# A Strassen-Winograd decoder step on 8 cores: new load order at the start, a gate/up epilogue without POOL, other weight slots, scheduler margins, and a reordered last stage before the odd mixer and the end

## The chip, the cores and the metric

The kernel runs on all 8 cores of one Trainium2 chip. Each core does the same work on its own data, and no core talks to another. The metric is the device time of the slowest core, in microseconds (us). Cores 0 to 3 are on one die, 4 to 7 on the other.

The program has a slower state that came in some executions: the cores of one die showed a lower granted TensorE clock than the others, and the time was some per cent longer. This document compares fast runs with fast runs only.

## The reference

One step of a two-layer decoder: a prompt group (8 sequences of 2048) and a sample group (128 sequences of 8 new tokens) share all weights.

```python
for layer in range(2):
    x = x + 0.5 * swiglu(rmsnorm(x), w_gate, w_up, w_down)      # FFN 1 (layer 0), FFN 3 (layer 1)
    h = rmsnorm(x)
    if layer == 0: m = even_mixer(h)     # chunked spatial gating || short gated convolution
    else:          m = odd_mixer(h)      # causal pooling over windows 2, 4, 8, 16
    x = x + m
    x = x + 0.5 * swiglu(rmsnorm(x), ...)                       # FFN 2, FFN 4
y = rmsnorm(x)
# D_MODEL 1024, D_FF 2816; swiglu(h) = (silu(h @ w_gate) * (h @ w_up)) @ w_down
```

Each core has one prompt sequence and 16 sample sequences, 2176 columns in all. They are handled as four token blocks of 544 columns. An FFN does two blocks at a time ("first half", "second half").

## The kernel before

Nearly all of the work is bf16 matmuls of 272 columns. Each 2x2 block of an FFN product is done with the seven products of Strassen-Winograd, M1 to M7, so DVE must form sums of weights ("S", four per weight item) and differences of activations ("T") before TensorE can use them.

```python
PARTS = [(0, 6), (6, 8), (14, 8)]     # the three column parts of a half of an FFN
def weight_sums(wt, n):               # 4 DVE operations of 128x1024 (gate/up): the "S" sums
    ...
def tsums(buf, o):                    # 3 DVE operations per 4 stored tiles: the "T" differences
    ...
```

Weights go through three slots of SBUF. A load into a slot can start only when the item that lay there has been released, so the assignment of items to slots, and the order of the cells that use them, decide how early a load starts.

```python
            k = (0, 0, 2, 0)[2 * l + w]
            for half in range(2):
                for pi, (f0, nf) in enumerate(PARTS):
                    for f in range(f0, f0 + nf, 2):
                        items.append((("gu", l, w, f, half), 4096, W0 + SLOT * (k % 3), SLOT))
                        k += 1
                    for q in range(2):
                        items.append((("dn", l, w, pi, q, half), nf * 512, W0 + SLOT * (k % 3), SLOT))
                        k += 1
                if (l, w, half) == (0, 1, 0):
                    k += 1
# ... in ffn(): the order of the gate/up cells (weight item i, token block t) of the last part
                if pi == 2:
                    cells[-6:] = [(i, t) for t in range(2) for i in range(n - 3, n)]
```

The epilogue of a gate/up cell (X is gate, Y is up). Two of the four products gate*up are formed by POOL:

```python
            X_.prod(7, X_.c, False)
            t22 = X_.sum5(X_.c)               # DVE: SBUF <- PSUM + M5
            X_.prod(3, X_.b, False)
            t12 = X_.sum5(X_.b)
            give(X_.b)
            Y_.prod(7, Y_.c, False)
            u22 = Y_.sum5(Y_.c)
            Y_.prod(3, Y_.b, False)
            u12 = Y_.sum5(Y_.b)
            give(Y_.b)
            act_silu(t=t22)
            act_silu(t=t12)
            self.put(B22, t22, u=u22)         # POOL: SBUF <- SBUF * SBUF
            self.put(T2B, t12, u=u12)         # POOL
```

A norm squares eight chunks on ACT, adds them on POOL, and sums over partitions with one TensorE matmul against ones. The `Down` cells at the end of an FFN go output half by output half (q outer, token block t inner).

The order of instructions on every engine is not written by hand. A list scheduler in the program simulates all engines with a cost formula for each operation, gives each operation a latest start LS worked out backwards from an ideal, gapless TensorE, and picks, with a few exceptions, the available operation with the smallest LS:

```python
            LS[i] = f - (issue(o) + dma_t(o) if o.ndma else o.cost)
            # ... when operation i has been placed, each successor s becomes ready:
                ready_t[s] = max(ready_t[s], o.end + self.lat(o, ops[s]))
```

At the start, the SP queue issues the four quarters of the first token block of x, and the small constants (norm gains) after them.

## Time and profile before

The median was 2232.51 us (4 runs, 2231.01 to 2233.3). The busy part of the page of the kernel before, core 0 (span, share of it, instructions):

```profile
span 2230.6 us, 53049 instructions; the slowest of 8 cores (2212.9 to 2230.6 us)
PE 2098.6 (94%) x16680; PEld 1631.1 (73%) x16712; DVE 1566.0 (70%) x3372; ACT 1228.9 (55%) x3070; POOL 987.4 (44%) x1150
```

TensorE is the limit: 2098.6 of 2230.6 us. What a change to other engines can win is the idle time of PE. The waits of PE in the kernel before name it, by the line of the waiting matmul and by what it waited for (total us, times, longest us). L785 is the main matmul, L1428 and L703 the norm sums, L662 the mixers' matmuls; L618 is the S sums, L756 the T differences, "arena<-wall" a weight load, L723 the multiplication that makes h, L905 the addition to x.

```profile
PE ps L1428 <- ACT accr L1426: 17.7, 3, 7.9
PE ps L703 <- POOL accr L693: 16.4, 10, 3.4
PE ps L785 <- DVE arena L618: 15.2, 12, 2.5
PE ps L785 <- DVE arena L756: 13.1, 8, 5.1
PE ps L785 <- DMA arena<-wall: 9.8, 8, 2.4
...
PE ps L662 <- DVE arena L723: 9.4, 3, 6.1
PE ps L785 <- DVE xT L905: 7.0, 12, 1.7
...
```

The following lines of the PE timeline of the kernel before (start, length, line, matmuls, and in brackets the idle time before them and its releaser) show places that the change aims at: the start (to 70 us), the weight loads near 950 us, and the norm before the odd mixer (1635 us).

```profile
27.34 1.83 PE L1428 MATMUL ps<-accr,onesr 128*128 128x272 f32 x5 [5.61 <-DVE accr L1423]
35.98 1.07 PE L785 MATMUL ps<-arena 128*128 128x272 bf16 x4 [5.07 <-DVE arena L756]
69.98 1.07 PE L785 MATMUL ps<-arena 128*128 128x272 bf16 x4 [3.69 <-DVE arena L723]
...
945.72 8.32 PE L785 MATMUL ps<-arena 128*128 128x272 bf16 x56 [2.03 <-DMA arena<-wall]
956.45 4.61 PE L785 MATMUL ps<-arena 128*128 128x272 bf16 x24 [2.41 <-DMA arena<-wall]
...
1635.79 4.41 PE L662 MATMUL ps<-arena 128*128 128x384 bf16 x16 [6.15 <-DVE arena L723]
```

The end, in the DVE timeline of the kernel before: all 16 multiplications of the last two token blocks stand in a row at the end, after the last main matmul (2210 us). The last matmul of all, a norm sum, ended at 2216.3 us.

```profile
2211.74 12.83 DVE L723 SCALAR_TENSOR_TENSOR xT<-xT,misc,arena 128x544 f32<-128x544 f32 x16 [1.10 <-ACT arena L713]
```

Two groups of the kernel before: POOL's multiplications, from the page, and the S sums on DVE, from the list of groups by form (count, busy us, mean ns, then idle time before and its releasers). DVE's own multiplications of this kind, 352 of them, took 437 ns.

```profile
L858 POOL TENSOR_TENSOR arena<-arena 128x272 bf16<-128x272 f32 x352 | 274.6, 792 | 681.8 <-ACT arena L840 476.6
```

```profile
L618 DVE TENSOR_TENSOR arena<-arena 128x1024 bf16<-128x1024 bf16 x240 | 197.0, 847 | 19.7 <-DMA arena<-wall 17.9
```

### The profile page before, as it was taken

What the parts mean: (1) busy time and instruction counts of PE and PEld (TensorE: products, weight loads), DVE (VectorE), ACT (ScalarE), POOL (GpSimd) and SP (SyncE); (2) the same over time, 40 slices, a digit from 0 to 9 for tenths busy, and PEclk for the clock granted to TensorE, in tenths of its full rate; (3) what the DMA queues carried; (4) which work ended last, traced back from release to release, by engine and by line L of the source; (5) the groups of instructions that cost most, each with busy time, mean ns of one, the idle gap of its engine ahead of it and who ended that gap; (6) DMA issues with size and microseconds to landing.
All of it is one profiled execution on the core that took longest, in us unless ns stands there. A gap on an engine that the chain in (4) does not pass through costs nothing.

```text
span 2230.6 us, 53049 instructions; the slowest of 8 cores (2212.9 to 2230.6 us)
## 1 busy us (share of the span) xinstructions
PE 2098.6 (94%) x16680; PEld 1631.1 (73%) x16712; DVE 1566.0 (70%) x3372; ACT 1228.9 (55%) x3070; POOL 987.4 (44%) x1150
## 2 busy tenths in 40 slices
PE   4799999999999999999999999999989999999995
PEld 3688788874555888778887887888744688878874
DVE  4777965577557877955587879655666887886665
ACT  3655565557334555555555555655565555555554
POOL 2633463356206423453345334633566533264325
PEclk9999999999999999999999999999999999999998
DMA  8587656561321676646555776565621277567563
GB/s 214 122 173 163 163 136 165 133 129 30 58 36 48 141 181 152 172 105 165 135 124 118 178 162 173 131 158 133 149 58 49 58 172 161 139 160 177 136 184 113
DMA packets 56290, 298.69 MB, mean 134 GB/s; under 512 B 7120, under 2 KB 11472, under 8 KB 31824
## 3 DMA queue, kind: packets, MB, share of 16 engines
q0 software_dynamic: 21600, 132.92, 35.7%
q1 hardware_dynamic: 34416, 162.38, 20.7%
q8 instruction: 140, 2.29, 0.4%
q14 instruction: 134, 1.10, 0.2%
HBM read 347.90 MB, written 80.28 MB: 192 GB/s over the span
## 4 chain that ended last, share of the span: by engine, by line
PE 75%; DVE 8%; DMA 5%; issue 5%; POOL 4%; ACT 2%; DVEq 0%; SPq 0%; POOLq 0%; ACTq 0%
PE ps L785 64%; PE ps L662 11%; DMA arena<-wall 3%; POOL arena L693 2%; DVE arena L723 2%; DVE arena L831 1%; DMA misc<-cst 1%; DVE arena L618 1%; DVE arena L756 1%; DVE arena L759 1%; DVE xT L905 1%; DMA arena<-scrgu 1%; POOL xT L925 1%; DVE xT L723 1%; ACT ps L806 0%
## 5 line engine op out<-in xcount | busy, mean ns | idle before, releaser
L785 PE MATMUL ps<-arena 128*128 128x272 bf16 x14784 | 1747.6, 281 | 62.1 <-DVE arena L618 15.2
L785 PEld LDWEIGHTS ps<-arena 128*128 128x128 bf16 x14784 | 1440.7, 98 | 365.0 <-issue 93.2
L806 ACT ACTIVATE ps<-ps 128x272 f32<-128x272 f32 x1088 | 416.7, 383 | 398.5 <-PE ps L785 237.1
L858 POOL TENSOR_TENSOR arena<-arena 128x272 bf16<-128x272 f32 x352 | 274.6, 792 | 681.8 <-ACT arena L840 476.6
L905 DVE SCALAR_TENSOR_TENSOR xT<-ps,xT 128x272 f32<-128x272 f32 x768 | 310.9, 435 | 138.2 <-PE ps L785 123.0
L662 PE MATMUL ps<-arena 128*128 128x512 bf16 (+2 forms) x1736 | 335.0, 351 | 14.3 <-DVE arena L723 9.4
L925 POOL TENSOR_TENSOR xT<-xT,arena 128x544 f32<-128x544 f32 x192 | 256.1, 1339 | 136.6 <-ACT arena L817 66.1
L831 DVE TENSOR_TENSOR arena<-ps,arena 128x272 f32<-128x272 f32 x704 | 294.2, 437 | 29.0 <-PE ps L785 16.3
L693 POOL TENSOR_TENSOR arena<-arena 128x272 f32<-128x272 f32 (+3 forms) x288 | 249.7, 873 | 118.1 <-DVE arena L723 28.4
L662 PEld LDWEIGHTS ps<-arena 128*128 128x128 bf16 x1768 | 171.6, 98 | 168.6 <-issue 17.6
L854 DVE TENSOR_TENSOR arena<-ps,arena 128x272 bf16<-128x272 f32 x352 | 153.7, 437 | 184.9 <-ACT ps L806 113.9
L840 ACT ACTIVATE arena<-arena 128x272 f32<-128x272 f32 x352 | 144.7, 427 | 196.4 <-DVE arena L831 191.8
L685 ACT ACTIVATE arena<-xT 128x272 f32<-128x272 f32 (+3 forms) x336 | 153.0, 457 | 163.2 <-POOL arena L693 95.3
L817 ACT ACTIVATE arena<-ps 128x272 f32<-128x272 f32 x544 | 214.4, 394 | 41.4 <-PE ps L785 26.1
L618 DVE TENSOR_TENSOR arena<-arena 128x1024 bf16<-128x1024 bf16 (+1 forms) x272 | 219.9, 833 | 21.3 <-DMA arena<-wall 19.4
L756 DVE TENSOR_TENSOR arena<-arena 128x544 bf16<-128x544 bf16 x240 | 127.7, 544 | 118.3 <-POOL arena L858 118.3
L723 DVE SCALAR_TENSOR_TENSOR arena<-xT,misc,arena 128x544 bf16<-128x544 f32 (+4 forms) x216 | 187.0, 895 | 7.5 <-ACT arena L713 3.9
L604 POOL DMA_DIRECT2D arena<-wall x148 | 87.0, 588 | 227.7 <-PE ps L785 104.4
L759 DVE TENSOR_TENSOR arena<-arena 128x272 bf16<-128x272 bf16 x480 | 157.0, 344 | 15.1
L840 ACT ACTIVATE arena<-ps 128x272 f32<-128x272 f32 x352 | 139.2, 395 | 14.3 <-PE ps L785 1.8
L1172 DVE TENSOR_TENSOR xT<-ps,xT 128x512 f32<-128x512 f32 (+2 forms) x80 | 48.2, 606 | 36.2 <-PE ps L662 35.9
L693 POOL TENSOR_TENSOR accr<-arena 128x272 fp32r<-128x272 f32 (+3 forms) x48 | 41.5, 864 | 10.2 <-DVE arena L756 2.7
(78 smaller groups left out, 532.9 us busy)
## 6 DMA issues: line engine op xcount, KB each, us to landing
arena<-wall POOLq DMA_DIRECT2D x68, 1024.0 KB, 10.4
arena<-wall POOLq DMA_DIRECT2D x72, 768.0 KB, 8.8
scrgu<-arena SPq DMA_DIRECT2D x44, 1024.0 KB, 8.9
arena<-scrgu SPq DMA_DIRECT2D x44, 1024.0 KB, 6.8
scrdn<-arena SPq DMA_DIRECT2D x16, 1024.0 KB, 7.6
arena<-scrdn SPq DMA_DIRECT2D x16, 1024.0 KB, 6.1
y<-xT SPq DMA_DIRECT2D x8, 1088.0 KB, 6.9
xT<-x SPq DMA_DIRECT2D x6, 1088.0 KB, 14.2
```

The source lines that it names most:

```text
L618: P.add("dve", lambda e, dst=dst, x=x, y=y, op=op: e.tensor_tensor(out=wt(*s(dst)), in0=wt(*s(x)), in1=wt(*s(y)), op=op), r=[wt.key(*s(x)) ...
L662: ins = e.matmul(banks[bk][:, 0:n], l, rr, start=(i == 0), stop=(i == len(pairs) - 1), skip_group_check=True)
L693: P.add("pool", lambda e: e.tensor_tensor(out=o, in0=acc(0, n), in1=q(0, n), op=ALU.add), r=[q.key(0, n), acc.key(0, n)], w=[ok], c=c_p(n))
L723: P.add("dve", lambda e: e.scalar_tensor_tensor(out=dst, in0=xc(c, a, n), scalar=g, in1=rs(a, a + n), op0=ALU.mult, op1=ALU.mult), r=[xck( ...
L785: ins = e.matmul(banks[bk][:, 0:N2], l, rr, start=fresh and kc == 0, stop=kc == self.nk - 1, skip_group_check=True)
L806: P.add("act", lambda e: e.activation(out=banks[dst][:, 0:N2], in_=banks[src][:, 0:N2], func=AF.Copy), r=[("ps", src)], w=[("ps", dst)], c ...
L817: P.add("act", lambda e: e.activation(out=s(0, N2), in_=banks[e_][:, 0:N2], func=AF.Copy, scale=0.5 if self.half else 1.0), r=[("ps", e_)] ...
L831: P.add("dve", lambda e: e.tensor_tensor(out=t(0, N2), in0=banks[bk][:, 0:N2], in1=s(0, N2), op=ALU.add), r=[("ps", bk), s.key(0, N2)], w= ...
L840: P.add("act", lambda e: e.activation(out=t(0, N2), in_=i_, func=AF.Silu), r=[r], w=[t.key(0, N2)], c=c_a(N2), tab="silu")
L858: P.add("pool", lambda e: e.tensor_tensor(out=m7(p, p + N2), in0=u(0, N2), in1=t(0, N2), op=ALU.mult), r=[u.key(0, N2), t.key(0, N2)], w=[ ...
L905: P.add("dve", lambda e: e.scalar_tensor_tensor(out=xc(dc, a, N2), in0=banks[bk][:, 0:N2], scalar=0.5, in1=xc(dc, a, N2), op0=ALU.mult, op ...
L925: P.add("pool", lambda e, dc=dc, a=a, s=s: e.tensor_tensor(out=x3[:, dc:dc + 2, a:a + N2], in0=x3[:, dc:dc + 2, a:a + N2], in1=s(0, N2).un ...
```

## The change

The change has six parts.

1. **Start.** The constants are loaded first, the second block of x is held until the first weights have landed, the later blocks until the third weight item has, and two stores of weight sums are held.
2. **Epilogue.** POOL's 352 multiplications go to DVE, which reads them from PSUM. For that the up-side sum is written back to PSUM.
3. **Weight slots and cell order.** Another slot map, and the last part of a half takes its last two items (not three) token block by token block.
4. **Margins.** The scheduler treats results that pass between engines (those for TensorE excepted) as ready up to 0.5 (ACT), 0.8 (DVE) or 1.5 us (POOL) later than computed, at most a quarter of the slack, so that it makes orders less tight.
5. **Before the odd mixer.** The last `Down` cells go token block by token block; of the last two token groups' eight squares, squares 4 to 7 are summed by TensorE directly rather than by POOL; three chunks of the mixer are interleaved at its start (two before); the pooling weights are loaded earlier.
6. **End.** The same token-major `Down` and direct sums in the last FFN, so that the third block's norm comes earlier.

The diff holds smaller things besides: a copy for the even mixer's bias moves from DVE to ACT, the norm sums get a fifth buffer, the first norms of the third and fourth block come later, and the scheduler has other cost figures for some DMAs.

The diff, cut to its core (`...` marks what is left out):

```diff
+    MARGIN = {"act": 500.0, "dve": 800.0, "pool": 1500.0}
...
-                ready_t[s] = max(ready_t[s], o.end + self.lat(o, ops[s]))
+                m = self.MARGIN.get(o.eng, 0.0) if ops[s].eng != "pe" and o.eng != ops[s].eng and not o.ndma else 0.0
+                f = o.end + self.lat(o, ops[s])
+                ready_t[s] = max(ready_t[s], f + max(0.0, min(m, (LS[s] + slip - f) * 0.25)))
...
-            k = (0, 0, 2, 0)[2 * l + w]
+            k = (0, 0, 1, 0)[2 * l + w]
...
-                        k += 1
+                        k += 2 if (l, w, half, f) in ((1, 0, 1, 6), (1, 0, 1, 14)) else 1
...
-                if (l, w, half) == (0, 1, 0):
-                    k += 1
...
+            if direct:
+                dq.append(lambda: self.sum(si, q, qk, i == 4, False))     # squares 4..7: TensorE adds them up
...
             Y_.prod(7, Y_.c, False)
-            u22 = Y_.sum5(Y_.c)
+            act_silu(t=t22)
+            Y_.sum5(Y_.c, Y_.a)                 # DVE: PSUM <- PSUM + M5
+            self.put(B22, t22, Y_.a)            # DVE: SBUF <- PSUM * SBUF
             Y_.prod(3, Y_.b, False)
-            u12 = Y_.sum5(Y_.b)
-            give(Y_.b)
-            act_silu(t=t22)
             act_silu(t=t12)
-            self.put(B22, t22, u=u22)
-            self.put(T2B, t12, u=u12)
+            Y_.sum5(Y_.b, Y_.b)
+            self.put(T2B, t12, Y_.b)
...
                 if pi == 2:
-                    cells[-6:] = [(i, t) for t in range(2) for i in range(n - 3, n)]
+                    cells[-4:] = [(i, t) for t in range(2) for i in range(n - 2, n)]
...
+                by_t = last and half == 1 and (mixer and l == 1 or final)
+                if by_t and nm_out.nidx != 1:
+                    nm_out.direct = {6: None, 7: None}
+                for q, t in [(0, 0), (1, 0), (0, 1), (1, 1)] if by_t else [(0, 0), (0, 1), (1, 0), (1, 1)]:
...
         for b in range(NB):
-            for k in range(2):
+            for k in range(3 if b < 2 else 2):
                 dc_block(k, order[k], b)
...
+    P.label = "const"
+    P.add("sp", lambda e: [e.dma_start(out=cT(0, 76), in_=cst)], w=[("cT",)], ndma=1, c=300.0, pri=-10.0, late=2000.0)
     P.label = "load x"
...
-    P.label = "const"
-    P.add("sp", lambda e: [e.dma_start(out=cT(0, 76), in_=cst)], w=[("cT",)], ndma=1)
-    pump(1, [xck(0, 0, 1)])
-    load_x(1, 0, [xck(7, N2, 1)])
-    pump(2, [xck(7, N2, 1)])
+    pump(1, [xck(0, 0, 1)], 2000.0)
+    pump(2, [xck(7, N2, 1)], 2000.0)
+    for c in range(0, NCH, 2):
+        load_x(1, c, 2, [wv(0).key(0, 1)])
...
```

## The prediction

> **What bounds the kernel now.** TensorE. The busy table gives PE 2098.6 us of a 2230.6 us span (94%), DVE 70%, ACT 55%, POOL 44%. In the windows table the steady stretches (334-446, 1003-1115, 1449-1561 us) have PE busy for all of their time. About 132 us are lost elsewhere: 114.5 us is idle time before matmuls (PE timeline), and 14 us follow the last matmul (2216.3 us). By place:
> - start, 0-112 us: 43.5 us idle. The chain of waits shows the small constants landing 21.6 us after their issue behind the x loads, blocking DVE until 25.8 us. Dense matmuls start at 36 us. A second hole at 50-72 us waits for the second token block's norm (POOL sums, h and T sums, about 9 us).
> - first half-ends of the FFNs: waits for weight sums (1.2-2.5 us each) and for weight DMA (4.4 us near 950 us).
> - before the odd mixer, 1595-1643 us: about 14 us, 6.15 of it one wait for h.
> - end, after 2190 us: about 9 us of gaps, then 16 final multiplies of 0.8 us in a row (2211.7-2224.6 us), then the store.
> The granted clock is 0.91 in the second slice, 0.94 at 1617-1672 us and 0.81 in the last: [...] here low clock and gaps coincide.
>
> **What the change does.**
> 1. Start: constants first, later x blocks held until the first weights land, two weight stores held. Dense matmuls at 24-28 us and a shorter second hole: -16 us (8 to 23).
> 2. Gate/up epilogue: 352 POOL multiplies (792 ns, 275 us of POOL) become DVE multiplies from PSUM (437 ns, +154 us). Off the path in steady stretches, this shortens the chain to the T sums, for which PE waits at the start of Down (13.1 us over 8 waits, 7.5 of it at the kernel's start): -4 us. [...] the weight sums take 688 ns at the start and 829 ns at 1230-1282 us, so I expect them shorter: DVE about 1670-1700 us busy, POOL about 710. But DVE at the half-ends is already 52-54 of 56 us, so new PE waits on DVE: +4 us.
> 3. Other weight slots, item order: -4 us. Scheduler margins: -2 us.
> 4. Odd mixer: three chunks interleaved, token-major Down, squares 4-7 summed by TensorE: -10 us. 16 more 272-column sums of 0.36 us over both uses: +4 us.
> 5. End: token-major Down puts half of the final multiplies before the end (6.4 us), and shortens the last norm's POOL chain: -10 us.
>
> Warmer clock: -4 us. Sum: -42 us. **Predicted 2190 us, 8 in 10 between 2168 and 2210. Faster by over 2%: 0.46; within 2%: 0.51; slower: 0.03.**
>
> **Right or wrong in the profile.** Start: dense matmuls from near 26 us. POOL multiply group gone, 704 DVE multiplies of about 437 ns, DVE busy under 1720 us. Odd: no 6 us gap for h. End: only 8 final multiplies after the last matmul. PE busy time about unchanged (2095-2105): the gain is idle time.
>
> **What would make it wrong.** DVE saturating in the first halves: PE gaps on DVE releasers growing by over 15 us. PSUM banks held longer. Start limited by the landing of x and first weights, not by constants. Mispredicted engine orders, so that holes move.

The sum: −16 − 4 + 4 − 4 − 2 − 10 + 4 − 10 − 4 = −42 us. "Warmer clock: -4 us" stands as the estimate from the low clocks listed (0.91, 0.94, 0.81).

## The result

The changed kernel took 2191.43 us (median of 9 runs, 2190.52 to 2356.37); the kernel before, 2233.01 us on the same chips (13 runs, 2229.33 to 2587.61). The ratio of fast runs is 0.9819, 95% interval 0.9809 to 0.9829: 1.8% less time, which counts as the same at a 2% limit. (A ratio here is the mean time of one kernel's fast runs over that of the other's of the same rounds, so it is not quite the ratio of the medians quoted.) The predicted 2190 us was met to 1.4 us. But a sum may be right with wrong terms, and here it was: that it came so close was luck, as the last part but one shows.

The page after, core 6:

```profile
span 2192.5 us, 53373 instructions; the slowest of 8 cores (2182.5 to 2192.5 us)
PE 2095.3 (96%) x16696; PEld 1636.9 (75%) x16728; DVE 1647.7 (75%) x3723; ACT 1231.1 (56%) x3071; POOL 696.0 (32%) x782
```

PE's busy time hardly moved (2098.6 to 2095.3 us), so nearly all of the gain is idle time of PE: by the medians of the 8 cores it fell from 129.0 to 91.6 us, 37.4 of the 38.8 us by which the median span fell. The waits of PE after, in the same columns (L832 is the main matmul now, L1483 and L743 the norm sums, L690 the mixers' matmuls; L953 is the addition to x, L638 the S sums, L803 the T differences, L1336 a pooling operation, L770 the multiplication that makes h):

```profile
PE ps L1483 <- ACT accr L1481: 17.6, 4, 8.5
PE ps L832 <- DVE xT L953: 12.3, 19, 1.4
PE ps L832 <- DVE arena L638: 9.0, 7, 2.4
PE ps L743 <- POOL accr L732: 8.1, 5, 2.7
PE ps L832 <- DVE arena L803: 7.5, 4, 5.5
PE ps L690 <- POOL arena L1336: 3.9, 1, 3.9
...
PE ps L690 <- DVE arena L770: 3.1, 2, 1.8
PE ps L832 <- DMA arena<-wall: 1.4, 1, 1.4
...
```

The waits for weight loads nearly went (9.8 to 1.4 us). Those for S sums, T differences and POOL's norm sums fell by about half. A wait for POOL in the odd mixer is new or longer (3.9 us; 1.8 us before), and those for additions to x grew from 7.0 to 12.3 us. The PE timeline after, at the start, at the end of the last FFN's gate/up work, and before the odd mixer:

```profile
21.87 1.44 PE L1483 MATMUL ps<-accr,onesr 128*128 128x272 f32 x4 [7.67 <-ACT accr L1481]
29.97 1.06 PE L832 MATMUL ps<-arena 128*128 128x272 bf16 x4 [5.50 <-DVE arena L803]
64.11 1.06 PE L832 MATMUL ps<-arena 128*128 128x272 bf16 x4 [3.44 <-DVE arena L770]
...
1611.21 24.82 PE L690 MATMUL ps<-arena 128*128 128x512 bf16 x134 [1.28 <-DVE arena L770]
1665.78 4.45 PE L690 MATMUL ps<-arena 128*128 128x512 bf16 x14 [3.89 <-POOL arena L1336]
...
2084.79 50.44 PE L832 MATMUL ps<-arena 128*128 128x272 bf16 x434
```

The constants no longer hold up DVE at the start: they landed 1.7 us after their issue, 21.6 us in the kernel before (list of DMA issues). The first norm sum that waits long is now that of the last quarter of x (21.87 us), and dense matmuls begin at 30 us on this core (36 us on the one shown of before). The hole of 6.15 us before the odd mixer is 1.28 us. The gate/up work of the last FFN runs 50 us without a gap. The end, in the DVE timeline after:

```profile
2169.86 0.78 DVE L770 SCALAR_TENSOR_TENSOR xT<-xT,misc,arena 128x544 f32<-128x544 f32 x1
2173.77 0.78 DVE L770 SCALAR_TENSOR_TENSOR xT<-xT,misc,arena 128x544 f32<-128x544 f32 x1
...
2176.87 9.98 DVE L770 SCALAR_TENSOR_TENSOR xT<-xT,misc,arena 128x544 f32<-128x544 f32 x14
```

Only two of the 16 multiplications moved ahead; 14 still stand in a row at the end. The groups of the epilogue after (list by form): POOL's multiplications are gone, DVE has 704 of them at 433 ns, and the S sums take 758 ns instead of 847.

```profile
L905 DVE TENSOR_TENSOR arena<-ps,arena 128x272 bf16<-128x272 f32 x704 | 294.0, 433 | 159.9 <-ACT ps L853 147.4 <-ACT arena L892 6.9 <-PE ps L832 3.3
L638 DVE TENSOR_TENSOR arena<-arena 128x1024 bf16<-128x1024 bf16 x240 | 177.8, 758 | 12.4 <-DMA arena<-wall 11.0 <-PE ps L690 0.2
```

### A table by stage

The two programs have the same 14,784 main matmuls in the same stages, so the start of the k-th main matmul marks the same place in both. The time between two marks is taken for each core of the profiled fast run, and the table gives the median of the 8 cores (so the stages add up to the span only within 0.4 us); it is worked out from the traces, and the places are chosen for what the change touches.

| stage (main matmuls) | before us | after us | after minus before |
|---|---|---|---|
| start (to 1,540) | 239.8 | 232.4 | −7.5 |
| half-end of FFN 2 (5,236 to 5,852) | 83.4 | 72.8 | −10.5 |
| last gate/up of FFN 4 (14,168 to 14,476) | 40.2 | 35.7 | −4.5 |
| half-ends of FFN 1 and FFN 4, first half of FFN 3 | 376.5 | 365.9 | −10.6 |
| even mixer, with FFN 1's last part (3,388 to 3,696) | 258.9 | 261.3 | +2.4 |
| odd mixer, with FFN 3's second half (9,240 to 11,088) | 363.5 | 361.6 | −2.0 |
| end (after 14,476) | 61.8 | 57.7 | −4.0 |
| everything else | 801.1 | 799.0 | −2.1 |
| whole span, median core | 2225.4 | 2186.6 | −38.8 |

Stretches whose instructions are the same in two kernels repeat within about 1 us (b_const below, which touches only the start, moved the stages after it, the last gate/up apart, by −0.2 to 0.0 us), with two exceptions. The start moves by up to 2.5 us from run to run (−2.3 us in u_tail, which does not touch it); over the cores of the kernel before, the last quarter of x landed at 12.9 to 24.6 us and dense matmuls began at 23.5 to 36.0 us. The last gate/up stage moves by up to 2 us where it waits for a load (39.5 to 43.4 us over the cores of the kernel before). Differences below that are not read.

Two stages, the half-end of FFN 2 and the last gate/up of FFN 4, hold 15.0 of 38.8 us. Together with the other half-ends and FFN 3's first half they hold 25.6 us. For all of that the prediction had a net 6 us (weight slots −4, margins −2, epilogue −4 and +4) and a share of the 4 us of "warmer clock".

### The profile page after: what moved, and what is told of

The parts are those of the page before. It is cut to its first block, busy times and chain, and to the rows that moved or that the text cites. A ratio compares the mean times of both kernels' runs of the same rounds, so it can differ in the third digit from the quotient of the medians.

```text
span 2192.5 us, 53373 instructions; the slowest of 8 cores (2182.5 to 2192.5 us)
## 1 busy us (share of the span) xinstructions
PE 2095.3 (96%) x16696; PEld 1636.9 (75%) x16728; DVE 1647.7 (75%) x3723; ACT 1231.1 (56%) x3071; POOL 696.0 (32%) x782
## 4 chain that ended last, share of the span: by engine, by line
PE 84%; DVE 5%; issue 3%; DMA 3%; POOL 3%; ACT 1%; DVEq 0%; SPq 0%; POOLq 0%; ACTq 0%
PE ps L832 72%; PE ps L690 11%; DMA arena<-wall 2%; POOL arena L732 1%; DVE arena L770 1%; DVE xT L953 1%; DMA xT<-x 1%; DVE arena L1327 1%; POOL xT L973 1%; DVE arena L638 0%; POOL arena L1331 0%; PE ps L743 0%; DVE arena L905 0%; DVE xT L770 0%; DMA cvv<-arena 0%
## 5 line engine op out<-in xcount | busy, mean ns | idle before, releaser
L832 PE MATMUL ps<-arena 128*128 128x272 bf16 x14784 | 1740.4, 280 | 43.9 <-DVE xT L953 12.3
L832 PEld LDWEIGHTS ps<-arena 128*128 128x128 bf16 x14784 | 1443.0, 98 | 334.8 <-issue 65.1
L953 DVE SCALAR_TENSOR_TENSOR xT<-ps,xT 128x272 f32<-128x272 f32 x768 | 312.6, 435 | 152.4 <-PE ps L832 132.4
L905 DVE TENSOR_TENSOR arena<-ps,arena 128x272 bf16<-128x272 f32 x704 | 294.0, 433 | 159.9 <-ACT ps L853 147.4
L690 PE MATMUL ps<-arena 128*128 128x512 bf16 (+2 forms) x1736 | 338.0, 353 | 10.7 <-POOL arena L1336 3.9
L690 PEld LDWEIGHTS ps<-arena 128*128 128x128 bf16 x1768 | 172.7, 99 | 167.3 <-issue 15.0
L732 POOL TENSOR_TENSOR arena<-arena 128x272 f32<-128x272 f32 (+3 forms) x272 | 233.1, 862 | 202.8 <-DVE arena L770 43.4
L638 DVE TENSOR_TENSOR arena<-arena 128x1024 bf16<-128x1024 bf16 (+1 forms) x272 | 195.2, 733 | 13.9 <-DMA arena<-wall 12.5
L721 ACT ACTIVATE arena<-xT 128x272 f32<-128x272 f32 (+3 forms) x320 | 143.9, 454 | 88.0 <-DVE xT L1232 50.3
L806 DVE TENSOR_TENSOR arena<-arena 128x272 bf16<-128x272 bf16 x480 | 171.8, 374 | 22.2 <-DVE arena L905 0.5
L770 DVE SCALAR_TENSOR_TENSOR arena<-xT,misc,arena 128x544 bf16<-128x544 f32 (+4 forms) x216 | 165.9, 797 | 14.6 <-PE ps L832 9.5
L883 DVE TENSOR_TENSOR arena<-ps,arena 128x272 f32<-128x272 f32 x352 | 151.2, 438 | 15.7 <-PE ps L832 13.4
L879 DVE TENSOR_TENSOR ps<-ps,arena 128x272 f32<-128x272 f32 x352 | 147.2, 446 | 12.1 <-PE ps L832 1.6
L803 DVE TENSOR_TENSOR arena<-arena 128x544 bf16<-128x544 bf16 x240 | 118.6, 506 | 10.7 <-DVE arena L905 0.5
L1232 DVE TENSOR_TENSOR xT<-ps,xT 128x512 f32<-128x512 f32 (+2 forms) x80 | 48.4, 607 | 39.8 <-PE ps L690 39.5
## 6 DMA issues: line engine op xcount, KB each, us to landing
arena<-wall POOLq DMA_DIRECT2D x68, 1024.0 KB, 10.5
```

What stands on the lines that cost most here:

```text
L638: P.add("dve", lambda e, dst=dst, x=x, y=y, op=op: e.tensor_tensor(out=wt(*s(dst)), in0=wt(*s(x)), in1=wt(*s(y)), op=op), r=[wt.key(*s(x)) ...
L690: ins = e.matmul(banks[bk][:, 0:n], l, rr, start=(i == 0), stop=(i == len(pairs) - 1), skip_group_check=True)
L732: P.add("pool", lambda e: e.tensor_tensor(out=o, in0=acc(0, n), in1=q, op=ALU.add), r=[qk, acc.key(0, n)], w=[ok], c=c_p(n))
L770: P.add("dve", lambda e: e.scalar_tensor_tensor(out=dst, in0=xc(c, a, n), scalar=g, in1=rs(a, a + n), op0=ALU.mult, op1=ALU.mult), r=[xck( ...
L806: P.add("dve", lambda e, dst=dst, x=x, y=y: e.tensor_tensor(out=q[:, dst], in0=q[:, x], in1=q[:, y], op=ALU.subtract), r=[buf.key(*s(x)), ...
L832: ins = e.matmul(banks[bk][:, 0:N2], l, rr, start=fresh and kc == 0, stop=kc == self.nk - 1, skip_group_check=True)
```

## The experiments

**Theories.** The first question was what the middle stages owe their gain to. *Theory of loads:* weights came late, and the new slots and cell order end that. Rivals: the gain is the epilogue (shorter chain to the T differences, shorter work on DVE), or the margins (sounder orders). The second question was whether the parts add up (theory "Sum": each alone is worth what it is worth in the whole) or lean on one another (theory "Lean": since one scheduler orders everything, a part helps only with the others). The third was what limits the start now: the order in which x and the first weights are issued ("O"), or the bytes that must land. The fourth was what became of the gain predicted for the odd mixer and the end.

Labels: `u_` is the changed kernel with one part undone, `b_` the kernel before with one part done alone, and the others go beyond the change. All 12 runs computed correct results. Times of one batch shared a chip and the runs of the kernel before on it. Chip 12 (the second batch) and chip 3 (the third) gave runs of the kernel before of 2257.89 to 2259.08 us besides those of 2228.85 to 2234.61 us, which makes the intervals of those ratios wide and, for a run that had no such execution itself, the ratio too low, by some 0.5% in the second batch and 0.2% in the third (b_const's 0.9906 is only −3.8 us by the profile's median core). The changed kernel was not run again in these batches, so a comparison "against after" is one across batches. The stage tables come from profiled fast runs in which all clocks were 0.984 or higher.

### First batch: undo one part

`u_six`: the old cell order only.

```diff
-                    cells[-4:] = [(i, t) for t in range(2) for i in range(n - 2, n)]
+                    cells[-6:] = [(i, t) for t in range(2) for i in range(n - 3, n)]
```

> The changed kernel with one line undone: the last part of each FFN half ends on six cells of three weight items, token block by token block, as before, in place of four cells of two items. Theory W (the gain in the FFN halves is weights that arrive in time, because two live items leave the third slot free for the next load): waits for weight DMA come back near the ends of the halves, the changed kernel loses 8 to 15 us of its gain of 41 us (2199 to 2206 us), of it 4 to 7 us in the last half of the last FFN. Theory E (the gain there comes from the gate/up epilogue, shorter DVE work and earlier T sums): less than 3 us (under 2194.5 us).

`u_slots`: the old slot map only.

```diff
-            k = (0, 0, 1, 0)[2 * l + w]
+            k = (0, 0, 2, 0)[2 * l + w]
...
-                        k += 2 if (l, w, half, f) in ((1, 0, 1, 6), (1, 0, 1, 14)) else 1
+                        k += 1
...
+                if (l, w, half) == (0, 1, 0):
+                    k += 1
```

> The changed kernel with the old map of weight items to the three slots (the skip of a slot at the half-end of the second FFN, start at slot 2). Theory W: at the half-end of the second FFN a load waits for a slot again, PE waits for weight DMA or weight sums there, 5 to 8 us lost between matmuls 5236 and 5852 of the 272-column ones, about 0 elsewhere: 2196 to 2200 us. Theory E: under 2 us.

`u_pool`: the old epilogue only (POOL multiplies again).

```diff
-            act_silu(t=t22)
-            Y_.sum5(Y_.c, Y_.a)
-            self.put(B22, t22, Y_.a)
+            u22 = Y_.sum5(Y_.c)
             Y_.prod(3, Y_.b, False)
+            u12 = Y_.sum5(Y_.b)
+            give(Y_.b)
+            act_silu(t=t22)
             act_silu(t=t12)
-            Y_.sum5(Y_.b, Y_.b)
-            self.put(T2B, t12, Y_.b)
+            self.put(B22, t22, u=u22)
+            self.put(T2B, t12, u=u12)
```

> The changed kernel with the old gate/up epilogue: two of four multiplies on POOL from SBUF, sums to SBUF. Theory E: 8 to 15 us lost, spread over the four FFNs, waits for the T sums back. Theory W: under 4 us lost (2191 to 2195 us), with DVE busy 75 to 90 us lower and POOL 275 us higher: work moved off the path. The prediction had put the net worth of this move at zero (-4 and +4).

`u_margin`: no margins.

```diff
-    MARGIN = {"act": 500.0, "dve": 800.0, "pool": 1500.0}
+    MARGIN = {}
```

> The changed kernel with the scheduler's margins set to nothing, all else kept. If the margins matter as the prediction said: 2 us lost (1 to 4), spread. If the engine orders depend on them more: 5 us or more lost, as waits on DVE or ACT at many places. If they do nothing: within 1 us.

**Measured.** The last three columns are stages of the profiled run against the changed kernel, in us.

| run | median us | ratio to before [95%] | median core | FFN 2 half-end | last gate/up FFN 4 | odd mixer |
|---|---|---|---|---|---|---|
| u_six | 2211.44 | 0.9910 [0.9888, 0.9932] | +20.4 | +0.4 | +7.0 | +8.3 |
| u_slots | 2207.10 | 0.9892 [0.9870, 0.9915] | +12.5 | +6.6 | 0.0 | +8.2 |
| u_pool | 2208.02 | 0.9895 [0.9869, 0.9922] | +12.9 | −0.5 | 0.0 | +3.5 |
| u_margin | 2292.47; its three fast runs 2206.33 to 2210.91 | 0.9898 [0.9868, 0.9927] | +15.6 | +2.2 | +0.1 | +7.0 |

Undoing the cell order brings back the whole loss of the last gate/up stage and more (+7.0 against the −4.5 of the change), and undoing the slot map brings back 6.6 of the 10.5 us at the half-end of FFN 2. Neither the epilogue nor the margins touch the former. The waits of PE in u_six show the loads again (1.4 us in the changed kernel), with the waits for S sums, which need the load, at 15.3 instead of 9.0 us:

```profile
PE ps L832 <- DVE arena L638: 15.3, 16, 2.6
PE ps L832 <- DMA arena<-wall: 9.5, 6, 3.1
```

u_pool loses 12.9 us, as theory E (the epilogue) expected (8 to 15) and theory W (the loads) did not (under 4): the epilogue has a worth of its own in the whole, spread over the FFNs and the odd mixer, besides that of the loads. With the multiplications back on POOL, the S sums take 860 ns in u_pool's groups by form (758 in the changed kernel), and the T differences wait 50.3 us in all for POOL's multiplications (L910):

```profile
L638 DVE TENSOR_TENSOR arena<-arena 128x1024 bf16<-128x1024 bf16 x240 | 201.7, 860 | 33.6 <-DMA arena<-wall 29.4 <-PE ps L690 1.4
L803 DVE TENSOR_TENSOR arena<-arena 128x544 bf16<-128x544 bf16 x240 | 132.6, 565 | 51.4 <-POOL arena L910 50.3
```

In u_slots a matmul of the odd mixer waits 3.5 us for a weight load. The odd mixer's stage gets worse in all four, also with parts that alone hardly move it (second batch); it takes in FFN 3's second half, where the slot map's two skips and one of the new cell orders lie. And the four losses sum to 61.4 us, where the whole change is worth 38.8. That speaks for Lean: a part's worth depends on the others. Undoing cannot tell how much a part is worth alone, so the next batch did parts alone.

### Second batch: do one part alone

`b_load`: the slot map and the cell order alone.

```diff
-            k = (0, 0, 2, 0)[2 * l + w]
+            k = (0, 0, 1, 0)[2 * l + w]
...
-                        k += 1
+                        k += 2 if (l, w, half, f) in ((1, 0, 1, 6), (1, 0, 1, 14)) else 1
...
-                if (l, w, half) == (0, 1, 0):
-                    k += 1
...
-                    cells[-6:] = [(i, t) for t in range(2) for i in range(n - 3, n)]
+                    cells[-4:] = [(i, t) for t in range(2) for i in range(n - 2, n)]
```

> The kernel before with only the new slot map and the shorter last group of cells. If weights that arrive late were a fault of the kernel before by itself, the waits for weight DMA near 950 and 2149 us go, 10 to 20 us are gained (2213 to 2223 us), most of it at the half-end of the second FFN and the end of the last. If the piece pays only together with the others (undoing both in the changed kernel cost 36 us in sum), under 5 us.

`b_dve`: the new epilogue alone (the epilogue lines of the diff above).

> The kernel before with only the new gate/up epilogue (all four multiplies on DVE from PSUM). If its worth is its own: 12 to 18 us gained, as undoing it cost 16.6 us. If it pays only with the new weight order and margins, or trades POOL waits for DVE waits as the prediction put it: within 4 us of the kernel before.

`b_margin`: the margins alone (the first lines of the diff above).

> The kernel before with only the scheduler's margins. If their worth is their own: 10 to 16 us gained, 2 us of it at each half-end of an FFN. If the margins were tuned to the other pieces: within 3 us, or slower.

`b_const`: the constants first, and nothing else of the start.

```diff
...
+            if o.first:
+                LS[i] = -1e9          # the scheduler puts it ahead of everything
...
+    P.label = "const"
+    P.add("sp", lambda e: [e.dma_start(out=cT(0, 76), in_=cst)], w=[("cT",)], ndma=1)
+    P.ops[-1].first = True
     P.label = "load x"
...
-    P.label = "const"
-    P.add("sp", lambda e: [e.dma_start(out=cT(0, 76), in_=cst)], w=[("cT",)], ndma=1)
```

> The kernel before with only the small constants sent first. If the constants bound the start (the prediction): the first dense matmul moves from 36 us to 28 us or less. If the last x block, landing near 20 us, and the chain behind it bind: it moves by 4 to 7 us to 29 to 32 us, and the second hole at 50 to 72 us keeps its length, so that 4 to 7 us remain at matmul 308.

**Measured.** Stages are against the kernel before.

| run | fast runs us | ratio [95%] | median core | start | FFN 2 half-end | last gate/up FFN 4 | other half-ends, FFN 3 | even mixer | odd mixer |
|---|---|---|---|---|---|---|---|---|---|
| b_load | 2210.45, 2211.07, 2232.84 | 0.9881 [0.9746, 1.0016] | −19.1 | −0.1 | −8.8 | −4.6 | −3.2 | −0.6 | −0.6 |
| b_dve | 2227.27, 2228.64, 2257.84 | 0.9953 [0.9834, 1.0073] | −2.3 | −0.7 | −0.4 | +0.7 | −2.9 | +1.0 | +0.1 |
| b_margin | 2246.87 to 2248.11, 2270.07 | 1.0021 [0.9930, 1.0111] | +12.2 | −1.7 | −1.9 | +1.9 | −0.5 | +2.8 | +7.9 |
| b_const | 2226.20 to 2229.08 | 0.9906 [0.9817, 0.9995] | −3.8 | −4.7 | −0.2 | +1.6 | −0.2 | 0.0 | 0.0 |

The ratio of b_load is unclear by its interval, but its profiled run (2211.07 us) and stage table are not: the two load stages account for 13.4 of its 19.1 us, and every one of the 8 cores took 74.6 us and 35.7 us in them (82.7 to 84.0 and 39.5 to 43.4 us before). In its waits of PE the loads are down from 9.8 to 2.0 us (one line moved by two):

```profile
PE ps L783 <- DMA arena<-wall: 2.0, 1, 2.0
```

**Why a wait of 2.03 us cost about 3.7.** In the windows view of the kernel before, core 0, each line is a stretch of 2 us with the busy times of PE, PEld, DVE, ACT and POOL, then the granted clock, the DMA share and GB/s. The wait for a load ends at 945.72 us.

```profile
944.00:946.00 2.00, 0.28 (x3) 0.27 (x4) 2.00 (x5) 0.86 (x2) 0.76 (x1) 1.00 0.13 36
946.00:948.00 2.00, 2.00 (x12) 1.39 (x11) 2.00 (x5) 0.78 (x2) 0.00 (x0) 0.56 0.90 295
948.00:950.00 2.00, 2.00 (x12) 1.39 (x11) 1.53 (x7) 0.00 (x0) 0.42 (x1) 0.58 0.53 221
950.00:952.00 2.00, 2.00 (x19) 1.69 (x18) 1.95 (x6) 1.75 (x6) 0.92 (x2) 1.00 0.73 65
```

PE is busy in all of the second and third stretch, but does 12 matmuls in each instead of 19, at a clock of 0.56 and 0.58. That loses (0.44 + 0.42) x 2 = 1.7 us more, so the wait of 2.03 us cost about 3.7. In the last FFN, core 2 had the longest wait for a load (PE timeline of the kernel before, core 2), and the same windows show a clock of 0.50 until 2149 us:

```profile
2143.69 1.06 PE L785 MATMUL ps<-arena 128*128 128x272 bf16 x4 [4.51 <-DMA arena<-wall]
```

```profile
2145.00:2147.00 2.00, 2.00 (x10) 1.33 (x10) 0.00 (x0) 0.65 (x3) 0.00 (x0) 0.50 0.00 0
2147.00:2149.00 2.00, 2.00 (x11) 1.33 (x10) 0.74 (x2) 0.53 (x2) 0.00 (x0) 0.50 0.00 0
```

This core took 43.4 us for the stage that takes 35.7 us without a wait: 7.7 us for an idle time of 4.5 us. Core 0 waited 1.44 us there and took 39.5 us. On core 0 the clock records show half the clock (0.50) for 3.41 us from 946.3 us on, 0.5 us after the end of the gap of 2.03 us, and in the last FFN for 3.41 us from 2151.2 us on, after gaps of 1.44 and 0.41 us within 1.1 us; on core 2 they show it for 6.83 us from 2142.7 us on, 1.0 us before the end of its wait.

A gap of such a length did not always go with half the clock. At the main matmul before which core 0 waited 2.41 us (at 956.45 us, with a clock of 0.52 from 958 to 960 us), core 4 waited 3.74 us for the same load, and its clock stayed at 1.00 (PE timeline, then windows view, kernel before, core 4):

```profile
947.22 2.94 PE L785 MATMUL ps<-arena 128*128 128x272 bf16 x24 [3.74 <-DMA arena<-wall]
```

```profile
948.00:950.00 2.00, 2.00 (x19) 1.58 (x17) 0.00 (x0) 1.02 (x3) 1.65 (x4) 1.00 0.03 8
```

The clock records of the traces before and after (8 cores each) show what went with the half clock. They hold two values, 1.00 and 0.50, and every stretch at one value but a core's last lasted a whole multiple of 3.41 us (1 to 457 times that). Cut at these places into slices of 3.41 us, from a core's first clock record to its last matmul, they give 9,951 slices at full clock. All 91 of these in which PE was busy for less than 40% of the time were followed by a slice at half; of the 52 with 40 to 50% 19 were, and of the 9,808 with more none. (Of the slices that reach beyond the last matmul, one with 65% was followed by half the clock as well.) Core 4's gap of 3.74 us was cut into 1.7 and 2.0 us by the border of two slices, in which PE was busy for 50% and 40% of the time. So a wait cost its own length alone here (core 4), or 1.7 us more (half of 3.41) for each slice at half the clock that followed and in which PE was busy throughout (core 0).

For the two load stages the theory of loads is thus shown from both sides: undone in the whole the new map and order lose there, done alone they gain.

b_margin fell against what the prediction had for it: alone, the margins cost 12.2 us, 7.9 of them in the odd mixer. b_dve is worth little alone. b_const confirms that the constants blocked DVE: five of eight cores start dense matmuls near 25 us (seven of the eight at 29 us or later before), but the gain that remains by matmul 1,540 is 4.7 us. The other three start at 27.7, 33.5 and 36.0 us; on these the last quarter of x landed at 17.1, 22.9 and 25.4 us, on the five at 13.8 to 14.7.

### Third batch: the parts together, the start, the odd mixer, the end

`b_three`: the kernel before with b_load, b_dve and b_margin together. If the parts add up, it is −19.1 − 2.3 + 12.2 = −9 us; if they lean on one another it comes close to the changed kernel outside the start, the odd mixer and the end.

> The kernel before with three pieces together: new slot map and last cells, new gate/up epilogue, scheduler margins. Alone, by the profiles' median core, they moved the end by -19, -2 and +12 us. Theory Sum (each has its own worth): about -9 us, a median core near 2216 us. Theory Lean (the margins suit only the new epilogue and the new weight order, as undoing them in the changed kernel cost 15 us): -22 to -30 us, a median core of 2195 to 2203 us; the start, the odd mixer and the end are then worth the remaining 9 to 17 us.

`s_gate`: the changed kernel, with the first weight load held until the last quarter of x has landed rather than the first.

```diff
-    pump(1, [xck(0, 0, 1)], 2000.0)
+    pump(1, [xck(7, N2, 1)], 2000.0)
```

> The changed kernel with the first weights sent only when the whole first x block has landed. Theory B (the start is bound by the bytes of x and of the first weights together, 4.2 MB at the 200 GB/s or so of the first 20 us): the last x quarter lands near 14 us in place of 21 us, but the weights land later, and dense matmuls still start at 28.5 to 32 us. Theory O (it is bound by the order: DVE and the squares stand behind the last x quarter): dense matmuls from 26 us or less.

The 200 GB/s in this is an estimate. The windows view has the cores at 182 to 192 GB/s over the first 20 us in the kernel before and at 165 to 175 in the changed one; from 5 to 20 us it is 197 to 214 in both.

`u_tail`: the changed kernel with the end undone.

```diff
-                by_t = last and half == 1 and (mixer and l == 1 or final)
+                by_t = last and half == 1 and mixer and l == 1
...
-                        flush(2)
-                        if final:
-                            nm_out.final(2)
+                        flush(2)
         if final:
+            flush(2)
+            nm_out.final(2)
             drain()
```

> The changed kernel with the end undone: last Down cells by column quarter first as before, squares of the last norm summed on POOL, final multiplies of the third token block after all of Down. If the end is worth what the traces' last stretch says: 3 to 6 us lost, all after matmul 14476, and TensorE's last matmul about 5 us later. If the multiplies had really moved ahead of the end, as the prediction said: 9 to 11 us lost.

`n_both`: the changed kernel with a third scan buffer in the odd mixer, and with the last four token groups (not two) summed by TensorE at the end, their norm sums issued one cell earlier.

```diff
...
-    Sb = [A.f32(S0 + 8256 + 2048 * i, 512) for i in range(2)]
+    Sb = [A.f32(S0 + 8256 + 2048 * i, 512) for i in range(2)] + [A.f32(N0 + 4096 + 2048 * 3, 512)]
...
-    wp = [A.f32(N0 + 4096 + 2048 * i, 512) for i in range(4)]
+    wp = [A.f32(N0 + 4096 + 2048 * i, 512) for i in range(3)]
...
-                    nm_out.direct = {6: None, 7: None}
+                    nm_out.direct = {k: None for k in ((4, 5, 6, 7) if final else (6, 7))}
...
-                    cell(Down(wv(j), nf, q, 2 * half + t, nm_out if last else None))
+                    early2 = by_t and final and (q, t) == (0, 1)
+                    cell(Down(wv(j), nf, q, 2 * half + t, nm_out if last else None), (lambda: (flush(2), nm_out.final(2))) if early2 else None)
```

> The changed kernel with two more edits, far apart in time. Odd mixer: a third buffer for the running sums (taken from the ring of scaled inputs, 4 to 3), so that a scan need not wait for POOL to read the one before the last. If the pooling chain of scan and POOL binds the odd mixer, the wait of 3.9 us for POOL before the projection shrinks to under 1.5 us, 2 to 4 us gained there; if POOL's own queue or the scans' sum bind it, under 1 us. End: all four last column segments summed by TensorE, and statistics of the third block taken before the main part of the next cell, so that its multiplies fill idle DVE time: 1 to 3 us gained, if 6 or more of the 16 multiplies come before the last matmul; none, if the 3 us of added sums cost as much. In sum 2185 to 2190 us.

**Measured.**

| run | fast runs us | ratio [95%] | median core | stage that it is about |
|---|---|---|---|---|
| b_three | 2208.40 to 2209.66 | 0.9869 [0.9778, 0.9959] | −23.7 against before | start −4.9, half-end of FFN 2 −10.6, last gate/up −4.5, other half-ends −10.9, even mixer +3.0, odd mixer +8.7 |
| s_gate | 2186.38 to 2187.72 | 0.9770 [0.9680, 0.9859] | −6.2 against after | start −6.2 |
| u_tail | 2194.08 to 2198.07 | 0.9810 [0.9720, 0.9901] | −0.5 against after | end +3.5 (and start −2.3, which it does not touch) |
| n_both | 2181.89 to 2186.04 | 0.9759 [0.9669, 0.9850] | −8.3 against after | odd mixer −4.2, end −1.9 |

*b_three* settles Sum against Lean: −23.7 us, not −9. At the half-ends and in the last gate/up stage it is the changed kernel to within 0.3 us. The half-ends other than FFN 2's are the clearest case: they gain 3.2, 2.9 and 0.5 us with one part each (6.6 in sum), and 10.9 us with all three. (4.9 of the 23.7 us lie in the start, where the sum has 2.5 and the difference is within the run-to-run range; without the start Lean still holds, −18.8 us for a sum of −6.7.) The two mixers do add up (odd +8.7 for a sum of +7.4, even +3.0 for +3.2). The odd mixer is the price: 8.7 us worse than before. The waits of PE in b_three from 1575 to 1700 us show what it consists of: additions to x (L908), h (L725), and a new wait for POOL's pooling (L1279).

```profile
PE ps L787 <- DVE xT L908: 6.3, 4, 2.5
PE ps L664 <- DVE arena L725: 5.7, 1, 5.7
PE ps L664 <- POOL arena L1279: 5.2, 1, 5.2
```

So the odd-mixer part of the change did what was predicted of it, and more than its net shows: from b_three to the changed kernel that stage falls from 372.2 us (363.5 + 8.7) to 361.6 us, about 11 us. But 9 of those repay what the other parts had cost there.

*s_gate* shows that the start was limited by order, and not by bytes alone. In the changed kernel the last quarter of x landed beside the first weights, so its squares were done only at 21 us. Held until x is there, the weights come a little later, but then nothing else is missing: on the 8 cores that quarter lands at 12.8 to 13.9 us (16.7 to 21.2 in the changed kernel), the first weights at 21.9 to 25.4 (19.1 to 21.0). In the PE timeline of s_gate, core 2, the last norm sum runs at 14.84 us, PE waits 9.07 us for the weights, and dense work follows with no wait for the T differences:

```profile
14.84 1.43 PE L1483 MATMUL ps<-accr,onesr 128*128 128x272 f32 x4 [0.33 <-ACT accr L1481]
25.34 0.39 PE L846 MATMUL ps<-arena 128*128 128x272 bf16 x1 [9.07 <-DMA arena<-wall]
```

Dense matmuls (from the fifth main matmul) start at 23.1 to 26.6 us on all 8 cores; it was 25.4 to 30.0 us. The weights come through POOL's queue and x through SP's; still, holding the one brought the landing of the other forward, from 16.7 to 21.2 us to 12.8 to 13.9.

*u_tail* gives the end's worth: +3.5 us over the last stage. Its median core shows nothing of it, because its start was 2.3 us luckier in that execution; its fast runs, 2194.08 to 2198.07 us against a median of 2191.43, do.

*n_both* beats both kernels. In its waits of PE the wait for POOL before the projection is 1.1 us (3.9 in the changed kernel), by a buffer more for the scan's results. The early norm sums put three multiplications ahead of the final row rather than two; 13 are left in it. The expectation had asked for six or more for a gain at the end, so what the end's 1.9 us come from is not shown.

```profile
PE ps L690 <- POOL arena L1338: 1.1, 1, 1.1
```

s_gate and n_both change different places and were not run together; whether they add up is left open.

## Why the prediction was right, and where it was wrong

The time was right: 2191.43 us for a predicted 2190, inside the range. That the gain would be PE's idle time and not its busy time was right, too (2095.3 us for 2095 to 2105). The terms, put by place:

| where | predicted us | measured us (stage table) |
|---|---|---|
| start | −16 | −7.5 |
| weight slots, item order, margins, epilogue (net), clock | −6 and −4 for the clock | −25.3 (−10.5 − 4.5 − 10.6 + 2.4 − 2.1) |
| odd mixer, with its half of the added sums | about −8 | −2.0 |
| end, with its half of the added sums | about −8 | −4.0 |

So the start, the odd mixer and the end fell short by 18.5 us in sum, and the rest gave 15.3 us more than predicted. That these cancel to within 3.2 us (−42 predicted, −38.8 measured) is luck.

**"Other weight slots, item order: -4 us" was the worst term.** Alone it is worth 19.1 us (b_load). Two readings were missed. First, the prediction took the idle time in front of a matmul as the cost of a late load; the trace shows the clock at half after such waits (for 3.41 us from 946.3 and again from 956.5 us on core 0, for 6.83 us from 2142.7 us on core 2), and the loss of the last gate/up stage was 7.7 us with a wait of 4.5 us (core 2) and 3.8 us with one of 1.44 (core 0). The prediction did count a warmer clock (−4 us), but for the whole kernel, not as a part of these waits; over the whole kernel it is worth about 2 us (PE was busy at half clock for 27.3 us before and 22.8 us after, medians of the cores; half of the difference). Second, it read one core: core 0, the slowest of the profiled execution, waited 1.44 us in the last FFN, the others took up to 43.4 us for the stage.

**"-16 us (8 to 23)" for the start failed in its limit.** Dense matmuls start at 25.4 to 30.0 us on the 8 cores, for "near 26 us". The constants did block DVE (b_const, −4.7 us), but behind them stood the next limit: the last quarter of x, delayed by the first weights. The prediction named this among what would make it wrong ("Start limited by the landing of x and first weights, not by constants"), and s_gate shows that removing it is worth 6.2 us more.

**"-4 us" for the shorter chain to the T sums, and "+4 us" for new waits of PE on DVE.** The net zero is about what the epilogue is worth alone (b_dve, −2.3 us). Its sizes were off in the good direction: DVE was busy 1647.7 us, not 1670 to 1700, because the S sums fell from 847 to 758 ns and the 128x544 multiplications that make h from 1066 to 904 ns; waits for S sums did not grow (15.2 us before, 9.0 after). The reason that the prediction gave is not shown by the traces. What they show: with the multiplications back on POOL (u_pool) the S sums take 860 ns again; in the kernel before, on all 8 cores, the 867 S sums of this size that overlap an instruction of POOL (DMA issues left out) took 1080 ns in the mean, and the 1,053 that do not 682 ns; in the changed kernel only 303 overlap one, at 1168 ns, and 1,617 do not, at 683 ns. POOL at 696 us was as predicted (710). New waits on DVE did come, for additions to x (7.0 to 12.3 us), about the predicted +4 us; that the epilogue causes them is not shown.

**"Scheduler margins: -2 us"** had the wrong sign for the part alone (b_margin, +12.2 us) and the wrong size in the whole (u_margin, +15.6 us when undone). Both are true, since the orders lean on one another. The prediction treated six parts as terms of a sum.

**"-10 us" for the odd mixer** was right in mechanism and near in size (about −11 us against b_three; the hole for h went from 6.15 to 1.28 us), but against the kernel before only −2.0 us remain. The prediction had no term for what the margins would cost in that stage (+7.9 alone, b_margin; +8.7 in b_three), nor for the 3.89 us wait for POOL before the projection.

**"token-major Down puts half of the final multiplies before the end (6.4 us)"** failed: 2 of 16 moved. The end gained 4.0 us by the other way that the prediction named, the shorter chain of the last norm: from the end of the last main matmul to the end of the last norm sum 1.8 us passed instead of 6.6 (medians of the cores), u_tail brings these 4.8 us back (it undoes the cell order and TensorE's adding of the last squares together, so which of the two did it is not told apart); from the last matmul of all on it took 14.6 us instead of 14.2. The trace shows the multiplications in a row after the additions to x, of which DVE had one every microsecond or so; why the scheduler did not place more of them in between was not tested.

**Open.** The even mixer's stage lost 2.4 us. b_margin (+2.8), perhaps b_dve (+1.0) and b_three (+3.0) show that these parts can do that, but taking either out of the changed kernel did not bring it back (−0.7 and +1.0 us). Its cause is not settled.

## What to carry to other kernels

A late load can cost TensorE more than the gap in front of the matmul (here about 3.7 us for a gap of 2.03, and 7.7 for one of 4.5): look at the granted clock in the 6 us after it (here half the clock ended 3.5 to 5.9 us after the gap), on more than one core, and count both. When one scheduler orders all engines, the parts of a change are not terms of a sum; do a part alone and undo it in the whole, and expect the two to differ. And when a block at the start is removed, ask what would have been late anyway: the next limit may be half of the predicted gain.
